# A two-layer encoder trunk on one core: order inside three norms, an adaLN rate, the kept outputs, the last transfers, and the queue of some rows

## The chip, the core and the metric

The kernel runs on one core of one Trainium2 chip. The engines named here are the TensorE (PE, matmuls; PEld is its weight load), the VectorE (DVE), the ScalarE (ACT), GpSimd (POOL) and SyncE (SP), which issues nearly all transfers. The metric is the device time of one execution in microseconds (us); lower is better. Differences of a few us are spoken of, so the runs are repeated.

## The reference

One sequence of 256 tokens, width 2048, two layers, everything in float32. In each layer a vector of six times 2048 values is made from a conditioning vector; its parts shift, scale and gate the two halves of the layer. Cut to what matters:

```python
for l in range(DEPTH):                                   # 2 layers
    mod = cond @ w_ada[l] + b_ada[l]                     # 2048 x 12288
    sh_a, sc_a, g_a, sh_m, sc_m, g_m = split(mod, 6)
    h = rmsnorm(x) * (1 + sc_a) + sh_a
    proj = h @ w_in[l]                                   # all attention inputs
    mix = concat(diff_attention(proj), mla_attention(proj)) @ w_o[l]
    x = x + g_a * mix
    h = rmsnorm(x) * (1 + sc_m) + sh_m
    y = square(relu(h @ w_mlp_in[l])) @ w_mlp_out[l]     # 2048 x 8192 x 2048
    x = x + g_m * y
return rmsnorm(x) * final_norm_g
```

The differential attention adds a bias that depends on the tokens' distance, the same in both layers.

## The kernel before

**Matmuls in parts.** Each weight tile is loaded raw, 1 MB or 768 KB at a time, into a ring of five tiles (`raw`, line 168). `part` (from line 145) makes two tiles of each half: ACT copies it at the precision that PE multiplies fast (`hi`, line 151), and DVE subtracts that from the raw half (`lo`, line 152). Four `hi` and four `lo` tiles exist. Activations are split in the same way. A product is then three matmuls: `hi` by high, `hi` by low and `lo` by high (lines 192 to 194 in `mac`, 213 and 216 in the wide form, 298, 299 and 301 for rows of output, 270 and 272 in `wide_by_k`). So each weight passes SP's queue, ACT and DVE before PE can use it, and the three engines' instructions stand in one fixed order each, mostly that in which the code is written. `behind(a, b)` puts instruction a behind b on its engine where a scheduler could choose otherwise.

**The adaLN rows.** `w_ada` comes as 192 tiles of 1 MB (`ada`, issued at line 346) that use the same ring of five. DVE multiplies each with the conditioning vector and sums it (line 362), 2.28 us apiece; lines 374 and 376 finish a piece of `mod`. How many are fetched beside the weights is set by rates: each call of `weights` adds `self.rate` to a credit and fetches a tile per whole credit (`more_ada`, line 157). The rates are one line of numbers (95); that of layer 0's attention, 1.1, holds through its value stage, the eight weights `w_dv` that `interleave` (line 976) mixes with the second attention. Where a stage needs a part of `mod` that isn't there, `ada_need` fetches and sums it at once.

**The norms.** The very first norm has a function of its own (`first_norm_then_by_k`); its loads, adaLN rows above all, fill the start of the program. The other three go through `norm_then_by_k` (line 707): layer 0's MLP (with `by_k`), layer 1's attention and layer 1's MLP (with `wide_by_k`). The 2048 columns of x are taken in eight pairs of 128. A pair is transposed by PE into a bank (`tx`, line 1125) and copied out (`xT`, line 1134 on ACT or 1132 on DVE); `modulated` scales it on DVE (`ht`, line 684), adds the shift on ACT (`h`, line 687: the high part) and makes the low part on DVE (line 688). Then PE multiplies the pair with its weight tiles into six banks that stay open over all eight pairs. Six banks, one for the norm's roots (`pn`) and one for the transposes make the eight banks of PSUM. In the code, pair 0's h is followed by its weight parts, by its matmuls, and by the transposes of pairs 6 and 7, before pair 1's h is written.

**The gates and the row.** `gate` (line 1061) writes a part of `mod`, one element per partition and column, to DRAM and reads it back as one row broadcast to all partitions, into `self.row` (its tile is called `bias` in the profile). Both transfers are issued on SP's queue (lines 1065 and 1067), the second behind the first one's landing. The same tile holds the attention's bias; layer 0 puts that aside in DRAM (`bias_kept`, line 960) and layer 1 fetches it (line 869). At line 962 x is loaded once more, into the tile that then takes the sums.

**The MLP's outputs.** The 8192 hidden columns are taken in four blocks (`fb`). Each has eight pairs of hidden tiles and then four chunks of 512 output columns for two halves of the tokens (`rows`, 298 to 301). `update` (lines 1076 and 1078) multiplies a result with the gate's row and adds it to x. In layer 0 the gate comes only with block 1, so block 0's eight results are kept (`late`) and go through `update` in one batch ahead of block 1's chunks. `final` (line 1028) does the last chunk of layer 1, the last norm and the output, half by half of the tokens: two scalings on DVE, one on ACT, and two transfers of 512 KB.

Of the kernel before, what the change touches and what calls it, by code (L numbers as in the profile page):

```python
# [16 lines left out]
P = 128  # L17
T = 256
D = 2048
# [78 lines left out]
RATE_A0, RATE_A1, RATE_A2, RATE_K, RATE_K1, RATE_M = 1.1, 0.5, 0.7, 0.6, 0.0, 0.66  # L98
# [3 lines left out]
class Trunk:  # L102
# [33 lines left out]
    def weights(self, src, width=2048):  # L136
        raw = self.raw(src, width)
        half = width // 2
        out = []
        for i in range(2):  # L140
            w, ins = self.part(raw, i, half)
            out.append(w)
        self.more_ada(ins)
        return out

    def part(self, raw, i, half, after=None):
# [4 lines left out]
        self.nc.scalar.activation(hi, v, AF.Copy)  # L151
# [37 lines left out]
    def mac(self, ps, w, c, m, x, first, last, shared=False):  # L189
# [4 lines left out]
        mm(ps, lo, x[0], start=False, stop=last, skip_group_check=shared)  # L194
# [34 lines left out]
    def by_k_weights(self, srcs, n, whole):  # L229

        out = []
        for src in srcs:
# [5 lines left out]
            else:  # L238
                w = self.weights(src, 2 * half)
# [3 lines left out]
    def by_k(self, banks, blocks, xs, k0, nk, n=4, whole=None):  # L243


        for b, (w, half) in enumerate(blocks):
            for i in range(len(w) * half // (n * P)):
                k = k0 + i
                for j in range(n):
# [7 lines left out]
                    else:  # L257
                        self.mac(ps, w[c // half], c % half, P, xs[k], first, last, True)

    def wide_by_k(self, banks, blocks, xs, k0, nk):  # L260
# [4 lines left out]
        for i in range(2 * half // (n * P)):  # L265
# [3 lines left out]
            for j, ps in enumerate(banks):  # L269
                mm(ps.rearrange("p a b -> p (a b)"), part(j, 0), both, start=k == 0, stop=False)  # L270
            for j, ps in enumerate(banks):
                mm(ps[:, 0], part(j, 1), x, start=False, stop=k == nk - 1)  # L272
# [404 lines left out]
    def modulated(self, x, r, k, sh, sc, after=None):  # L677
# [4 lines left out]
        for i, (hi, lo, _) in enumerate(out):  # L682
            c = slice(k + i, k + i + 1)
            ins = nc.vector.scalar_tensor_tensor(t[:, i], x[:, i], sc[:, c], r, ALU.mult, ALU.mult)
            if after is not None:
                self.behind(ins, after)
            self.last_h = nc.scalar.activation(hi, t[:, i], AF.Identity, bias=sh[:, c])  # L687
            ins = nc.vector.scalar_tensor_tensor(lo, t[:, i], sh[:, c], hi.bitcast(F32), ALU.add, ALU.subtract)  # L688
# [18 lines left out]
    def norm_then_by_k(self, l, sh, sc, src):  # L707
# [17 lines left out]
        late = self.last_spread  # L725
        banks = None
        h = []
        for p in range(8):
# [3 lines left out]
            new, ins = self.modulated(x[p], rb, k, self.mod[l, sh], self.mod[l, sc], ins if p == 1 else None)  # L732
            h += new
            if p == 0:
                x += [self.turned(p, late, False, self.last_h) for p in range(4, 6)]
                banks = self.open_banks(6)
            if p:
                blocks = self.by_k_weights([src[p, b] for b in range(2 - l)], 6, False)
            else:
# [5 lines left out]
                blocks = [(parts[2 * b : 2 * b + 2], 768) for b in range(len(raws))]  # L745
            if l == 0:
# [3 lines left out]
            if p == 0:  # L750
                x += [self.turned(p, late) for p in range(6, 8)]
# [630 lines left out]
```

## Time and profile before

| what | value |
|---|---|
| runs shown, median (lowest to highest) | 2208.36 us (2207.84 to 2215.34), 3 runs |
| profiled execution, its own time | 2209.65 us |
| its span from the first instruction to the last | 2207.8 us |
| mean granted clock of TensorE | 0.994 |
| TensorE busy | 2155.4 us |
| VectorE, ScalarE, GpSimd busy | 1595.2, 1143.0 and 1.9 us |
| bytes moved | 594.76 MB, 269 GB/s on the mean |

A row of the timeline gives start and duration in us, the engine, the line of the code, the operation, the output and inputs by name (buffer numbers left out), the shape, how many of them follow one another, and in brackets how long the engine sat idle before and what ended that. A row of waits gives the waiting engine, its output and line, the instruction waited for, then total us, times, and the longest. A row of a stretch gives from:to, the length, then busy us (and instructions) of PE, PEld, DVE, ACT and POOL, the granted clock, the share of the DMA engines and GB/s. Starts of the timeline lie on the axis of the span.

### The profile page before, as it was taken

How to read it: one execution, taken by the hardware profiler on the slowest of the kernel's cores; microseconds unless marked ns; L12 is line 12 of the kernel's file. 1: busy time of each engine (PE TensorE's matmuls, PEld its weight loads, DVE VectorE, ACT ScalarE, POOL GpSimd, SP SyncE). 2: the span in 40 equal slices, each digit the busy share in tenths (PEclk: the TensorE clock that was granted, in tenths of full speed). 3: DMA queues.
4: the chain of work that ended last, by engine and by line, in shares of the span. 5: the costliest groups of instructions: out<-in, count | busy, mean ns of one | idle time of the engine just before them, and what ended most of it. 6: DMA issues, size and time to landing. Idle time of an engine off the chain costs nothing.

```text
span 2207.8 us, 29335 instructions
## 1 busy us (share of the span) xinstructions
PE 2155.4 (98%) x11498; PEld 1865.6 (84%) x11498; DVE 1595.2 (72%) x2122; ACT 1143.0 (52%) x1722; POOL 1.9 (0%) x10
## 2 busy tenths in 40 slices
PE   7999999999999999999999999999999999999998
PEld 6898878888887888888879998888888888888886
DVE  7888778988678878887876876778755555555555
ACT  6555664555454355345454565546545534644643
POOL 0000000000000000000000000000000000000000
PEclk9999999999999999999999999999999999999999
DMA  9988889798887888888967776666875555555552
GB/s 388 421 333 324 269 312 348 277 348 324 321 291 284 339 305 320 326 307 304 333 218 251 260 254 218 251 237 228 282 287 194 191 192 189 191 193 188 191 196 91
DMA packets 94795, 594.76 MB, mean 269 GB/s; under 512 B 17984, under 2 KB 18368, under 8 KB 27840
## 3 DMA queue, kind: packets, MB, share of 16 engines
q1 hardware_dynamic: 94656, 592.88, 73.7%
q8 instruction: 90, 1.47, 0.2%
q14 instruction: 49, 0.40, 0.1%
HBM read 589.66 MB, written 3.18 MB: 269 GB/s over the span
## 4 chain that ended last, share of the span: by engine, by line
PE 91%; DVE 4%; DMA 3%; ACT 1%; issue 1%; SPq 0%; DVEq 0%; ACTq 0%
PE ps L213 18%; PE pr L301 13%; PE pr L298 13%; PE pr L299 13%; PE ps L216 9%; PE pk L256 3%; PE pk L270 2%; PE pk L193 2%; PE pk L194 2%; PE pk L192 2%; PE pv L283 1%; PE pv L282 1%; PE pv L281 1%; PE pk L272 1%; DVE ada L362 1%; DMA raw<-in_w_m 1%
## 5 line engine op out<-in xcount | busy, mean ns | idle before, releaser
L152 DVE TENSOR_TENSOR lo<-raw,hi 128x1024 fp32r<-128x1024 f32 (+1 forms) x714 | 835.0, 1193 | 464.3 <-issue 219.3
L151 ACT ACTIVATE hi<-raw 128x1024 fp32r<-128x1024 f32 (+1 forms) x714 | 733.5, 1036 | 743.1 <-PE pr L299 363.8
L362 DVE SCALAR_TENSOR_TENSOR ada<-ada,cond 128x2048 f32<-128x2048 f32 x192 | 437.9, 2283 | 12.1 <-DMA ada<-in_w_ada 11.4
L213 PE MATMUL ps<-h,hi 128*128 128x512 f32 x1856 | 431.8, 390 | 2.4 <-ACT hi L151 2.4
L213 PEld LDWEIGHTS ps<-h,hi 128*128 128x128 f32 x1856 | 345.1, 188 | 72.2 <-ACT hi L151 2.8
L298 PE MATMUL pr<-hi,hid 128*128 128x512 f32 x1024 | 398.9, 390 | 0.0
L299 PE MATMUL pr<-hi,hid 128*128 128x512 f32 x1024 | 398.7, 389 | 0.0
L301 PE MATMUL pr<-lo,hid 128*128 128x512 f32 x1024 | 254.5, 390 | 5.2 <-DVE lo L152 5.2
L216 PEld LDWEIGHTS ps<-h,lo 128*128 128x128 f32 x1856 | 230.3, 192 | 4.5
L216 PE MATMUL ps<-h,lo 128*128 128x256 f32 x1856 | 231.7, 283 | 0.0
L301 PEld LDWEIGHTS pr<-lo,hid 128*128 128x128 f32 x1024 | 192.5, 188 | 45.7 <-DVE lo L152 5.8
L298 PEld LDWEIGHTS pr<-hi,hid 128*128 128x128 f32 x1024 | 192.5, 188 | 40.3 <-ACT hi L151 0.4
L299 PEld LDWEIGHTS pr<-hi,hid 128*128 128x128 f32 x1024 | 192.4, 188 | 39.8
L1144 ACT ACTIVATE sum<-ps 128x256 f32<-128x256 f32 x110 | 41.7, 381 | 102.2 <-PE ps L216 101.5
L192 PE MATMUL pk<-h,hi 128*128 128x256 f32 x320 | 89.2, 287 | 5.0 <-ACT h L687 5.0
L193 PE MATMUL pk<-h,hi 128*128 128x256 f32 x320 | 91.0, 286 | 0.3 <-DVE h L688 0.3
L194 PE MATMUL pk<-h,lo 128*128 128x256 f32 x320 | 90.8, 286 | 0.0
L256 PE MATMUL pk<-hf,w 128*128 128x256 f32 x384 | 83.9, 379 | 0.0
L256 PEld LDWEIGHTS pk<-hf,w 128*128 128x128 f32 x384 | 72.8, 190 | 9.9
L186 DVE TENSOR_TENSOR hid<-relu,hid 128x256 fp32r<-128x256 f32 x128 | 48.2, 419 | 43.3 <-ACT hid L185 43.3
L1076 DVE TENSOR_TENSOR yg<-pr,bias 128x512 f32<-128x512 f32 x72 | 47.5, 682 | 30.0 <-PE pr L301 30.0
L192 PEld LDWEIGHTS pk<-h,hi 128*128 128x128 f32 x320 | 60.9, 193 | 5.7 <-ACT h L687 5.6
(230 smaller groups left out, 2486.4 us busy)
## 6 DMA issues: line engine op xcount, KB each, us to landing
raw<-in_w_m SPq DMA_DIRECT2D x238, 1024.0 KB, 5.3
ada<-in_w_ada SPq DMA_DIRECT2D x192, 1024.0 KB, 6.2
raw<-in_w_o SPq DMA_DIRECT2D x32, 1024.0 KB, 5.8
raw<-in_w_m SPq DMA_DIRECT2D x24, 768.0 KB, 5.5
raw<-in_w_dv SPq DMA_DIRECT2D x16, 1024.0 KB, 6.2
raw<-in_w_t SPq DMA_DIRECT2D x12, 1024.0 KB, 4.9
w<-in_w_a SPq DMA_DIRECT2D x24, 384.0 KB, 13.5
raw<-in_w_a SPq DMA_DIRECT2D x12, 768.0 KB, 5.4
```

Of the source, the lines that this page charges most:

```text
L151: self.nc.scalar.activation(hi, v, AF.Copy)
L152: ins = self.nc.vector.tensor_tensor(lo, v, hi.bitcast(F32), ALU.subtract)
L192: mm(ps, hi, x[0], start=first, stop=False, skip_group_check=shared)
L193: mm(ps, hi, x[1], start=False, stop=False, skip_group_check=shared)
L194: mm(ps, lo, x[0], start=False, stop=last, skip_group_check=shared)
L213: mm(ps.rearrange("p a b -> p (a b)"), part(w, k, 0), x[2], start=k == 0, stop=False)
L216: mm(ps[:, 0], part(w, k, 1), x[0], start=False, stop=k == nk - 1)
L256: self.nc.tensor.matmul(ps, v, whole[k], start=first, stop=last, skip_group_check=True)
L298: mm(ps, xh[:, c], part(i, 0), start=kq == 0 and i == 0, stop=False)
L299: mm(ps, xl[:, c], part(i, 0), start=False, stop=False)
L301: self.last_mm = mm(ps, xh[:, c], part(i, 1), start=False, stop=kq == 3 and i == 3)
L362: ins = nc.vector.scalar_tensor_tensor(w, w, 1.0, self.cond, ALU.mult, ALU.mult, accum_out=acc[:, i : i + 1])
```

## The change

The change has five parts.

1. In `norm_then_by_k` the h of pair 1 is ordered ahead of the later weight parts on ACT and DVE; the transposes of pairs 6 and 7 move behind the first column of matmuls of pairs 1 and 2; and `wide_by_k` begins its very first product with the `lo` matmuls.
2. The value stage of layer 0 has a rate of its own, 1.6.
3. The kept outputs are no longer updated in a batch: each of block 1's chunks adds the kept one to its own result (`added`), and updates once.
4. `final` does both halves' sums first and writes four transfers of 256 KB a half, two of the eight from ACT's queue.
5. The gates' rows, the bias that is kept and fetched, and the reload of x are issued on GpSimd's queue.

```diff
-RATE_A0, RATE_A1, RATE_A2, RATE_K, RATE_K1, RATE_M = 1.1, 0.5, 0.7, 0.6, 0.0, 0.66
+RATE_A0, RATE_V, RATE_A1, RATE_A2, RATE_K, RATE_K1, RATE_M = 1.1, 1.6, 0.5, 0.7, 0.6, 0.0, 0.66
...
+        if l == 0:
+            self.rate = RATE_V
         self.interleave(
             [val(cg, kq) for cg in range(2) for kq in range(4)],
             mla[6:] + [av[0][0], av[1][0]],
         )
+        if l == 0:
+            self.rate = RATE_A0
...
     def part(self, raw, i, half, after=None, hi_after=None):
...
-        self.nc.scalar.activation(hi, v, AF.Copy)
+        ins = self.nc.scalar.activation(hi, v, AF.Copy)
+        if hi_after is not None:
+            self.behind(ins, hi_after)
...
         for p in range(8):
...
-            new, ins = self.modulated(x[p], rb, k, self.mod[l, sh], self.mod[l, sc], ins if p == 1 else None)
+            new, ins = self.modulated(x[p], rb, k, self.mod[l, sh], self.mod[l, sc], gate)
+            gate = None
...
+                gate = ins, self.last_turn
...
+                order = (self.last_h, ins) if p == 1 else None
+                blocks = self.by_k_weights([src[p, b] for b in range(2 - l)], 6, False, order)
+            if p in (1, 2):
+                x.append(self.turned(5 + p, self.last_mm, False, self.last_h))
...
-            if p == 0:
-                x += [self.turned(p, late) for p in range(6, 8)]
...
-            for j, ps in enumerate(banks):
-                mm(ps.rearrange("p a b -> p (a b)"), part(j, 0), both, start=k == 0, stop=False)
-            for j, ps in enumerate(banks):
-                mm(ps[:, 0], part(j, 1), x, start=False, stop=k == nk - 1)
+            for h in (1, 0) if k == 0 else (0, 1):
+                for j, ps in enumerate(banks):
+                    if h:
+                        mm(ps[:, 0], part(j, 1), x, start=k == 0, stop=k == nk - 1, skip_group_check=True)
...
-            for n, y in enumerate(late):
-                self.update(y.rearrange("p a b -> p (a b)"), n % 2, n // 2)
-            late = []
...
+                    if late:
+                        pss = [self.added(late.pop(0), ps) for ps in pss]
                     self.updates(pss, c, end)
...
+    def added(self, y, ps):
+
+        self.nc.vector.tensor_tensor(y, ps, y, ALU.add)
+        return y
...
-            nc.scalar.activation(self.xr[:, t, :1024], self.xr[:, t, :1024], AF.Copy, scale=r)
-            nc.sync.dma_start(out[:, :1024], self.xr[:, t, :1024])
...
-            nc.sync.dma_start(out[:, 1024:], self.xr[:, t, 1024:])
+            parts = [self.xs_of(t, i) for i in range(4)]
+            outs = [self.io["out"][t, :, 512 * i : 512 * i + 512] for i in range(4)]
+            ins = nc.vector.tensor_scalar(parts[2], parts[2], r, None, ALU.mult)
+            self.behind(ins, ready[1] if t else self.last_x)
+            nc.sync.dma_start(outs[2], parts[2])
...
+            nc.sync.dma_start(outs[3], parts[3])
+            for i in range(2):
+                nc.scalar.activation(parts[i], parts[i], AF.Copy, scale=r)
+                (nc.scalar if t else nc.sync).dma_start(outs[i], parts[i])
...
-        self.nc.sync.dma_start(d.rearrange("k p -> p k"), self.mod[l, g])
+        self.nc.gpsimd.dma_start(d.rearrange("k p -> p k"), self.mod[l, g])
...
-        self.nc.sync.dma_start(self.row, flat.broadcast_to([P, D]))
+        self.nc.gpsimd.dma_start(self.row, flat.broadcast_to([P, D]))
```

The same replacement of `nc.sync` by `nc.gpsimd` is made for `bias_kept` (both ways) and for the two halves of x.

In the norm of layer 0's MLP, ACT's rows behind pair 0's h (the last of it is `h_3570` before and `h_3584` after) read as follows before; `xT` are transposed pairs, `hi` the later weight parts, `h_3700` and `h_3701` pair 1's h:

```order
L687 ACTIVATE h_3570<-ht_3568,mod_81 128x256
L1134 ACTIVATE xT_3582<-tx_3577 128x512
L1134 ACTIVATE xT_3589<-tx_3584 128x512
L151 ACTIVATE hi_3710<-raw_3708 128x768
L151 ACTIVATE hi_3714<-raw_3708 128x768
L151 ACTIVATE hi_3721<-raw_3719 128x768
L151 ACTIVATE hi_3725<-raw_3719 128x768
L1134 ACTIVATE xT_3690<-tx_3685 128x512
L1134 ACTIVATE xT_3697<-tx_3692 128x512
L687 ACTIVATE h_3700<-ht_3699,mod_81 128x256
L687 ACTIVATE h_3701<-ht_3699,mod_81 128x256
```

and after the change:

```order
L698 ACTIVATE h_3584<-ht_3582,mod_81 128x256
L1165 ACTIVATE xT_3596<-tx_3591 128x512
L1165 ACTIVATE xT_3603<-tx_3598 128x512
L698 ACTIVATE h_3700<-ht_3699,mod_81 128x256
L698 ACTIVATE h_3701<-ht_3699,mod_81 128x256
L151 ACTIVATE hi_3710<-raw_3708 128x768
L151 ACTIVATE hi_3714<-raw_3708 128x768
L151 ACTIVATE hi_3721<-raw_3719 128x768
L151 ACTIVATE hi_3725<-raw_3719 128x768
L1165 ACTIVATE xT_3736<-tx_3731 128x512
L698 ACTIVATE h_3811<-ht_3810,mod_81 128x256
```

Pair 1's h moved ahead of four weight parts and of the copies of two transposed pairs, of which one now stands between those parts and pair 2's h (`h_3811`), the other further on.

On DVE the kept outputs (`y`) stood, before, between the two halves' `lo` of one weight tile at the start of block 1's chunks. The first ten rows, behind which nine more updates follow before the next `lo`:

```order
L152 TENSOR_TENSOR lo_6214<-raw_6211,hi_6213 128x1024
L1076 TENSOR_TENSOR yg_6150<-y_4852,bias 128x512
L1076 TENSOR_TENSOR yg_6153<-y_4854,bias 128x512
L1078 TENSOR_TENSOR x<-x,yg_6150 128x512
L186 TENSOR_TENSOR hid_6141<-relu_6138,hid_6141 128x256
L186 TENSOR_TENSOR hid_6142<-relu_6138,hid_6142 128x256
L1078 TENSOR_TENSOR x<-x,yg_6153 128x512
L1076 TENSOR_TENSOR yg_6156<-y_5003,bias 128x512
L1076 TENSOR_TENSOR yg_6159<-y_5005,bias 128x512
L1078 TENSOR_TENSOR x<-x,yg_6156 128x512
```

After the change, the end of the first of the four chunks:

```order
L154 TENSOR_TENSOR lo_6352<-raw_6349,hi_6351 128x1024
L1047 TENSOR_TENSOR y_4859<-pr_6157,y_4859 128x512
L1047 TENSOR_TENSOR y_4861<-pr_6158,y_4861 128x512
L1107 TENSOR_TENSOR yg_6305<-y_4859,bias 128x512
L1107 TENSOR_TENSOR yg_6308<-y_4861,bias 128x512
L1109 TENSOR_TENSOR x<-x,yg_6305 128x512
L1109 TENSOR_TENSOR x<-x,yg_6308 128x512
L154 TENSOR_TENSOR lo_6356<-raw_6349,hi_6355 128x1024
```

The sixteen instructions of the batch are gone, and each chunk has two more, the additions, ahead of its four.

At the program's end DVE's rows before (`rms` is the reciprocal root of a half, `cond` holds the final norm's weights):

```order
L1109 RECIPROCAL rms_18157<-rms_18157 128x1
L1047 SCALAR_TENSOR_TENSOR x<-x,rms_18157,cond 128x512
L1049 TENSOR_SCALAR x<-x,rms_18157 128x512
L1076 TENSOR_TENSOR yg_18625<-pr_18473,bias 128x512
L1078 TENSOR_TENSOR x<-x,yg_18625 128x512
L1109 RECIPROCAL rms_18157<-rms_18157 128x1
```

and after:

```order
L1140 RECIPROCAL rms_18141<-rms_18141 128x1
L1107 TENSOR_TENSOR yg_18604<-pr_18457,bias 128x512
L1109 TENSOR_TENSOR x<-x,yg_18604 128x512
L1071 TENSOR_SCALAR x<-x,rms_18141 128x512
L1074 SCALAR_TENSOR_TENSOR x<-x,rms_18141,cond 128x512
L1140 RECIPROCAL rms_18141<-rms_18141 128x1
```

The second half's update moved ahead of the first half's two scalings.

More of the change, by code (lines that the diff above doesn't have):

```diff
@@ L140, in weights @@
         for i in range(2):
-            w, ins = self.part(raw, i, half)
+            w, ins = self.part(raw, i, half, order and order[1], order and order[0])
             out.append(w)
@@ L144, in weights, with part @@
         return out
-    def part(self, raw, i, half, after=None):
+    def part(self, raw, i, half, after=None, hi_after=None):
         v = raw[:, i * half : (i + 1) * half]
@@ L238, in by_k_weights @@
             else:
-                w = self.weights(src, 2 * half)
+                w = self.weights(src, 2 * half, order)
             out.append((w, half))
@@ L258, in by_k @@
                         self.mac(ps, w[c // half], c % half, P, xs[k], first, last, True)
+                if i == 0 and not whole:
+                    self.last_mm = self.last_mac
     def wide_by_k(self, banks, blocks, xs, k0, nk):
```

51 lines of the change are left out of this document (30 added, 21 removed).

## The prediction

> **What bounds the kernel now.** I read the page's busy times and chain first, then the waits of the TensorE (PE), then the timeline around each of those waits. The page, busy us with the share of the span, and the chain that ended last:
>
> ```profile
> PE 2155.4 (98%) x11498; PEld 1865.6 (84%) x11498; DVE 1595.2 (72%) x2122; ACT 1143.0 (52%) x1722; POOL 1.9 (0%) x10
> PE 91%; DVE 4%; DMA 3%; ACT 1%; issue 1%; SPq 0%; DVEq 0%; ACTq 0%
> ```
>
> PE is busy for 98% of 2207.8 us and carries 91% of the chain. The matmuls stay as they are, so the change can win only from the 52.4 us in which PE idles (2207.8 less 2155.4) and from time at a lower clock. PE's waits (total us, times, longest), those that the change can touch:
>
> ```profile
> PE pr L301 <- DVE lo L152: 5.2, 1, 5.2
> PE pk L192 <- ACT h L687: 5.0, 3, 3.6
> PE pk L270 <- DVE h L688: 4.7, 4, 1.6
> PE ps L213 <- ACT hi L151: 2.4, 1, 2.4
> PE psm L1267 <- DVE sm L1269: 2.1, 2, 1.6
> PE pss L192 <- ACT hi L151: 2.1, 1, 2.1
> ```
>
> They are single waits, each with a place of its own. I went through them in the timeline (start, duration, instruction, idle before it).
>
> **Part 1, the norms ahead of a projection.** Norm of layer 0's MLP, layer 1's attention and layer 1's MLP, PE's rows at the second and third pair:
>
> ```profile
> 420.21 0.66 PE L1125 MATMUL tx<-ident,x 128*128 128x128 f32 x4 [0.86 <-ACT xT L1134]
> 421.95 0.98 PE L192 MATMUL pk<-h,hi 128*128 128x256 f32 x6 [1.08 <-ACT h L687]
> 1140.46 1.67 PE L270 MATMUL pk<-h,hi 128*128 128x512 f32 x6 [0.76 <-DVE h L688]
> 1146.07 0.66 PE L1125 MATMUL tx<-ident,x 128*128 128x128 f32 x4 [0.69 <-ACT xT L1134]
> 1148.33 2.93 PE L270 MATMUL pk<-h,hi 128*128 128x512 f32 x6 [1.60 <-DVE h L688]
> 1495.26 0.66 PE L1125 MATMUL tx<-ident,x 128*128 128x128 f32 x4 [0.69 <-ACT xT L1134]
> 1497.52 1.65 PE L270 MATMUL pk<-h,hi 128*128 128x512 f32 x6 [1.60 <-DVE h L688]
> ```
>
> In all three the transposes of pairs 6 and 7 stand between pair 0 and pair 1, the second waits for ACT to clear its bank, and pair 1 waits for its h, which ACT and DVE reach only after the weight parts. Afterwards the transposes lie one behind each of pairs 1 and 2, and h goes first, so both waits go. Layer 0's MLP: 0.86 + 1.08 = 1.9. Layer 1's attention: 0.69 + 1.60 = 2.3, and the six matmuls took 2.93 where the same six at 1497.52 took 1.65: the clock had dropped, 1.3 more. The 0.76 at pair 0 waits for the low half of h; the changed order begins with six matmuls that read the high half alone, taken at 0.6. Sum 4.2. Layer 1's MLP: 0.69 + 1.60 + 0.6 = 2.9, but the order keeps a sum of one adaLN row ahead of pair 1's scaling:
>
> ```profile
> 1490.78 2.28 DVE L362 SCALAR_TENSOR_TENSOR ada<-ada,cond 128x2048 f32<-128x2048 f32 x1
> ```
>
> It ends at 1493.06, and ht, h on ACT and h on DVE, of 0.4 to 0.5 each, need some 2 us more. PE is through with pair 0 about 1494, since it waits from 1494.57 with four transposes done. About 1.0 is late again; 1.9 is left. The weight parts that now come later are next in line on both engines. They are needed one product after h, so I count nothing for them and cover them in the slack term below.
>
> **Part 2, four more adaLN rows in layer 0's value stage.** Later they need not be forced. Where they are forced now, at pair 7 of the MLP's norm, PE stops:
>
> ```profile
> 477.73 0.86 PE L192 MATMUL pk<-h,hi 128*128 128x256 f32 x5 [3.65 <-ACT h L687]
> 470.00:480.00 10.00, 6.10 (x45) 5.69 (x44) 10.00 (x16) 4.07 (x6) 0.00 (x0) 0.94 0.98 401
> ```
>
> The second row is a stretch: its length, then busy us of PE, weight load, DVE, ACT and POOL, clock, share of the DMA engines, GB/s. DVE is busy for all ten us, with the forced sums, and the clock is at 0.94 on the mean because it drops behind the stop; I price the drop at 1.5 by the one in part 3, whose matmuls can be counted out. Gain 3.7 + 1.5 = 5.2. The price lies in the value stage, a row of the same kind:
>
> ```profile
> 240.00:297.00 57.00, 55.38 (x268) 46.23 (x267) 40.16 (x65) 31.85 (x63) 0.00 (x0) 1.00 0.87 290
> 90.00:120.00 30.00, 30.00 (x144) 26.52 (x143) 18.91 (x27) 6.46 (x12) 0.00 (x0) 1.00 1.02 420
> ```
>
> Four sums of 2.28 lift DVE from 40.2 to 49.3 of 57 us, and four loads of 1.05 MB lift DMA from 290 to 364 GB/s, under the 420 of the second row. Both fit on average, not at each point: cost from 0 (a mere filling of gaps) to 5 (half of the 9.1 us on PE's path), taken at 1, nearer to the gaps.
>
> **Part 3, the kept outputs.** Now sixteen DVE instructions stand in one batch ahead of a weight part for which PE waits:
>
> ```profile
> 692.98 1.29 DVE L1076 TENSOR_TENSOR yg<-y,bias 128x512 f32<-128x512 f32 x2
> 703.39 2.35 DVE L152 TENSOR_TENSOR lo<-raw,hi 128x1024 fp32r<-128x1024 f32 x2
> 704.66 2.08 PE L301 MATMUL pr<-lo,hid 128*128 128x512 f32 x4 [5.19 <-DVE lo L152]
> 706.53 0.63 PE L298 MATMUL pr<-hi,hid 128*128 128x512 f32 x1
> 727.00:749.00 22.00, 22.00 (x99) 18.22 (x98) 18.05 (x19) 8.56 (x9) 0.00 (x0) 1.00 0.90 341
> ```
>
> The wait of 5.19 goes. The four matmuls behind it took 1.87 to the next start against four times the usual 0.225 (22 us by 98 to 99 matmuls), so 1.0 is lost to the clock there, and the matmul after them still shows a long 0.63: 1.5 in all, an estimate. Gain 6.7. In return each chunk of the next feed-forward block gets two additions of about 0.65: DVE goes from 18.05 to 19.4 of the 22 us that a chunk takes, 88%. Cost 0 to 4, taken at 0.5.
>
> **Part 4, the rows off SyncE's queue.** A gate is written out in pieces of 4 bytes and read back; until it has landed, the weight loads behind it crawl. The DMA issues from 610 to 640 (KB each, us to landing), the chain there, PE behind it, the page's row for all such loads, and SyncE's wait:
>
> ```profile
> gate<-mod SPq DMA_DIRECT2D x1, 8.0 KB, 14.2
> 622.20 13.86 DMA raw<-in_w_m
> 637.27 3.92 PE L213 MATMUL ps<-h,hi 128*128 128x512 f32 x16 [2.39 <-ACT hi L151]
> raw<-in_w_m SPq DMA_DIRECT2D x238, 1024.0 KB, 5.3
> SPq L1067 <- DMA gate<-mod: 14.5, 2, 7.7
> ```
>
> 8 KB take 14.2 us and a 1 MB load beside them 13.86, where the median of such loads is 5.3; PE loses 2.4. The same at the first gate costs the 1.6 of the psm wait. Taken from SyncE's ring, I expect the weights to flow past: 4.0.
>
> The bias, kept aside, and the reload of x go along, and no longer stand behind the weight loads of the attention stage. By their own waits (a normed chunk of pair 3, the bias's last write, the last normed chunk) they are free within the first norm, where the second row of part 2 has a DMA share of 1.02. Three transfers of 1.05 MB are 3.15 MB; at 420 GB/s that is 7.5 us of queue ahead of the last adaLN rows of the norm:
>
> ```profile
> 101.62 2.29 DVE L362 SCALAR_TENSOR_TENSOR ada<-ada,cond 128x2048 f32<-128x2048 f32 x1 [7.42 <-DMA ada<-in_w_ada]
> 119.19 0.96 DVE L152 TENSOR_TENSOR lo<-raw,hi 128x768 fp32r<-128x768 f32 x1 [3.11 <-issue]
> 129.22 0.16 DVE L374 SCALAR_TENSOR_TENSOR mod<-macc,vec 128x2 f32<-128x2 f32 x1
> 134.29 0.47 PE L192 MATMUL pk<-h,hi 128*128 128x256 f32 x1
> ```
>
> DVE already waits 7.42 for a row there, and PE begins pair 7 five us after mod with no gap. So lateness of mod shows: 0 (DVE has other pauses to give up) to 9 (7.5 and a clock drop of 1.5). I take 3: with its second pause of 3.1 DVE can make up a part, and a part of the loads waits for buffers anyway.
>
> On GpSimd's queue the clearing of kr now stands behind the return of the kept bias; layer 1's whole first norm lies between that return and the attention that reads both, so I count nothing.
>
> **Part 5, the end**, with DVE and SyncE behind PE's last matmul:
>
> ```profile
> 2197.82 0.75 DVE L1047 SCALAR_TENSOR_TENSOR x<-x,rms,cond 128x512 f32<-128x512 f32 x1
> 2198.89 0.68 DVE L1076 TENSOR_TENSOR yg<-pr,bias 128x512 f32<-128x512 f32 x1
> 2203.21 0.38 SPq L1050 DMA_DIRECT2D out_y<-x  x1
> ```
>
> yg of the second half waits on DVE behind two scalings of the first; now it goes first, 1.07 earlier (2198.89 less 2197.82). The last issue moves 256 KB instead of 512, and from it to the span's end 4.6 us pass now. From 0.5 (half of the move is kept) to 2.3 (the move, and a quarter of the 4.6): 1.6.
>
> **The attention stage of layer 0** is reshuffled by the scheduler: the weight parts stand ahead of two copies on ACT now.
>
> ```profile
> 215.29 0.39 PE L192 MATMUL pss<-lath,hi 128*128 128x256 f32 x1 [2.12 <-ACT hi L151]
> ```
>
> 2.1 plus 1.5 of clock are at stake; other rows may get late, so half: 2 (0 to 4).
>
> **The sum.** Gains: 1.9 + 4.2 + 1.9 + 5.2 + 6.7 + 4.0 + 1.6 + 2 = 27.5. Costs: 1 + 0.5 + 3 = 4.5. A stall that goes exposes the next late thing, as the 1.0 in layer 1's MLP norm; 0.4 for each of seven other places is 3. Net 20. The profiled execution is 2209.65 (span 2207.8 and 1.85 around it), which gives 2189.5; the median of the runs shown is 1.3 lower, so I forecast 2188.
>
> **Rivals.** *The gaps are filled again* (0.18): the feed-forward block at 88% DVE costs its 4, the value stage its 5, the first norm its 9. 27.5 − 18 − 3 = 6.5 is left, 2202: between faster and no change.
>
> *The gate stays a brake* (0.12): if the 4-byte pieces slow the 16 engines themselves and not SyncE's ring, moving them changes nothing. For it: DMA engines that serve both. Against it: SyncE's own wait of 7.7. The 4.0 go, so 2192. The Trainium skill, "DMA: Bandwidth & Descriptors", section "Issuing engines are not separate DMA queues", speaks for this rival: transfers run on the same 16 engines whoever starts them, and a second issuer saves only issue time. By it the sum would be 16 instead of 20; the 14.2 us for 8 KB fit it as well.
>
> *Slower: GpSimd's queue starves* (0.05). The place is the last gate:
>
> ```profile
> L1065 SPq DMA_DIRECT2D gate<-mod x4: 377/407/427, 256.3 to 1584.8; - x4
> 1607.78 1.28 DVE L1076 TENSOR_TENSOR yg<-pr,bias 128x512 f32<-128x512 f32 x2
> ```
>
> From 1584.8 to the first use of the row at 1607.78 are 23 us for two transfers in a row; 9.1 us less of sums ahead (four of 2.28) may give up to 9 more. If GpSimd's two transfers take over 32 us, yg blocks DVE and all weight parts behind it. It must take 32 + 31 = 63 us to eat the 20 and make it 11 slower: 2219.5. Against it: only this row is so near to its use. Nothing in the trace shows GpSimd moving anything, so the price is unknown. The Trainium skill, "SBUF — State Buffer", section "SBUF: two separate sides", warns that GpSimd can't write its descriptors during certain two-port DVE operations; no run here shows it yet.
>
> *Not what it says* (0.05): pair 1's order holds in the listing but h still comes late, because the transposed x of pair 1 or its adaLN rows end last. Part 1 falls from 8.0 to 2: 2194.
>
> **How the numbers follow.** My forecast has 0.60. 0.5% is 11.0 us, about what a measurement of this kernel can tell from no change: faster is below 2197.3, slower above 2219.4. Faster: 0.60, the 0.12 and 0.05 of the two small losses, and none of the refilled gaps, less 0.04 for my sum being too rich: 0.73. Same takes the 0.18, that 0.04 and a half of the starving case: 0.24. Slower: 0.03. The range: at the low end the costs at zero and attention at 4, 27.5 + 2 = 29.5, a little short of it, 2180; at the high end the refilled gaps at 2202 and some loss beyond, 2205.
>
> **What would show it.** Right: the waits at L301, L192 and L270 above gone, no adaLN sum ahead of pair 7, no 13-us weight load near 622, PE's idle near 30 us. Wrong: a new PE wait between 110 and 140; DVE waiting for a row near 1600; waits of PE for lo in the value stage or the next feed-forward block; PE idle as long as before.

## The result and the profile after

The changed kernel takes 2194.63 us (median of 4 runs, 2193.98 to 2199.35) against 2209.89 for the kernel before (4 runs beside them): the ratio is 0.9932, 95% interval 0.9908 to 0.9955. That is 15 us faster; 20 were forecast, and 2194.6 lies in the forecast range of 2180 to 2205. The profiled execution took 2194.0 with a span of 2191.8, which is 16.0 less than the span before.

The page, PE's share and the chain, and PE's waits after the change (as before: total us, times, longest):

```profile
PE 2148.8 (98%) x11498; PEld 1861.3 (85%) x11498; DVE 1590.6 (73%) x2114; ACT 1141.8 (52%) x1724; POOL 11.1 (1%) x22
PE 89%; DMA 5%; DVE 4%; ACT 1%; issue 1%; SPq 0%; ACTq 0%; DVEq 0%
```

```profile
PE psm L1298 <- DVE sm L1300: 6.1, 2, 5.6
PE pk L258 <- DMA w<-in_w_d: 3.6, 2, 2.3
PE psc L1232 <- ACT k L339: 1.5, 1, 1.5
PE pk L278 <- ACT hi L151: 1.3, 1, 1.3
PE pr L309 <- ACT hi L151: 1.0, 1, 1.0
PE ps L215 <- ACT hi L151: 0.8, 2, 0.4
```

The waits of 5.2, 5.0, 4.7 and 2.4 that the forecast had listed, and that of pss with 2.1, are gone or down to 0.8 and less; that of psm has grown. The largest new ones are a wait of 5.6 in the value stage, two for `w_d` in the first norm, and one of 1.5 for a key in the attention stage. PE's busy time fell too, by 6.6: behind the start, and ahead of the end, the granted clock dropped four times before (at 215, 478, 705 and 1148) and drops once now (at 275), and slow matmuls count as busy. PE's idle time is 43.0 (2191.8 less 2148.8), against 52.4 before and the "near 30" that the forecast named as a sign of being right.

To see where the 16.0 lie, I took the start of the same instruction in both traces at eight places. The difference after minus before, and its step from place to place, beside the forecast's terms for that stretch:

| up to | before | after | difference | step | forecast |
|---|---|---|---|---|---|
| first pkr matmul (keys; behind the first norm) | 150.12 | 154.40 | +4.3 | +4.3 | +3 |
| first pv matmul (value stage begins) | 225.90 | 226.24 | +0.3 | −3.9 | −2 |
| last pv matmul of layer 0 | 307.92 | 314.75 | +6.8 | +6.5 | +1 −1.6 |
| last update of the output projection | 405.68 | 413.72 | +8.0 | +1.2 | 0 |
| first update in block 1 of the MLP (the batch's, before, excepted) | 718.42 | 710.52 | −7.9 | −15.9 | −15.7 |
| pn, layer 1's first norm | 1138.34 | 1129.66 | −8.7 | −0.8 | 0 |
| last update of layer 1's projection | 1484.78 | 1471.36 | −13.4 | −4.7 | −4.2 |
| second chunk's update in layer 1's block 0 | 1626.74 | 1611.39 | −15.35 | −1.9 | −1.9 |
| end of the span | 2207.8 | 2191.8 | −16.0 | −0.65 | −1.6 |

The three norms, the forced rows and the kept outputs came out almost to the microsecond. What went wrong lies ahead of the MLP, between 0 and 414 us: there the change lost 8.0, where the forecast's terms (+3 −2 −0.6) made 0.4.

The value stage first. The chain there, GpSimd's queue, and PE at its stop:

```profile
257.31 2.21 DVE ada L373 x2
259.52 0.03 DVE r L1222
259.55 14.59 DMA raw<-in_w_dv
```

```profile
257.61 1.18 POOL L1096 DMA_DIRECT2D gate<-mod  x1 [137.72 <-DVE mod L387]
273.49 0.54 POOL L1098 DMA_DIRECT2D bias<-gate  x1 [14.70 <-DMA gate<-mod]
```

```profile
276.93 1.22 PE L1298 MATMUL psm<-kn,qn 128*128 128x256 f32 x2 [5.61 <-DVE sm L1300]
```

The gate's 8 KB go out at 257.6, now from GpSimd's queue; the weight load issued two us later takes 14.59, lands at 274.14, and all that wait for it stand behind it: `hi`, `lo`, the softmax's reduction on DVE, PE. The gate still is a brake. The first norm, PE's rows for the early part of `w_d`:

```profile
97.63 2.61 PE L258 MATMUL pk<-hf,w 128*128 128x256 f32 x11 [2.27 <-DMA w<-in_w_d]
131.98 7.17 PE L258 MATMUL pk<-hf,w 128*128 128x256 f32 x32 [1.31 <-DMA w<-in_w_d]
```

They follow the transfers of x and of the bias, which GpSimd issued at 66.18, 88.51 and 118.82. At the end DVE, ACT's queue and SyncE, the counterpart of the rows shown of before:

```profile
2182.45 0.69 DVE L1107 TENSOR_TENSOR yg<-pr,bias 128x512 f32<-128x512 f32 x1
2185.18 1.34 ACT L1080 ACTIVATE x<-x,rms 128x512 f32<-128x512 f32 x2 [0.23 <-DVE rms L1140]
2185.94 0.97 ACTq L1081 DMA_DIRECT2D out_y<-x  x2
2186.36 0.33 SPq L1078 DMA_DIRECT2D out_y<-x  x1
```

PE's last matmul ends at 2182.42, so the second half's update follows at once, and the last SyncE issue lies 3.94 behind PE where it lay 5.44 behind. But from it to the end of the span 5.4 us pass instead of 4.6.

### The profile page after: what moved, and what is told of

It is laid out like the page before. It is cut to its first block, busy times and chain, and to the rows that moved or that the text cites. A ratio compares the mean times of both kernels' runs of the same rounds, so it can differ in the third digit from the quotient of the medians.

```text
span 2191.8 us, 29356 instructions
## 1 busy us (share of the span) xinstructions
PE 2148.8 (98%) x11498; PEld 1861.3 (85%) x11498; DVE 1590.6 (73%) x2114; ACT 1141.8 (52%) x1724; POOL 11.1 (1%) x22
## 2 busy tenths in 40 slices
DMA packets 87307, 594.76 MB, mean 271 GB/s; under 512 B 9984, under 2 KB 10368, under 8 KB 20352
## 4 chain that ended last, share of the span: by engine, by line
PE 89%; DMA 5%; DVE 4%; ACT 1%; issue 1%; SPq 0%; ACTq 0%; DVEq 0%
PE ps L215 18%; PE pr L309 13%; PE pr L310 13%; PE pr L312 13%; PE ps L218 9%; PE pk L258 2%; PE pk L278 2%; PE pk L194 2%; PE pk L195 2%; PE pk L196 2%; DMA raw<-in_w_m 2%; DVE ada L373 1%; PE pv L293 1%; PE pv L294 1%; PE pv L292 1%; DMA w<-in_w_d 1%
## 5 line engine op out<-in xcount | busy, mean ns | idle before, releaser
L1107 DVE TENSOR_TENSOR yg<-pr,bias 128x512 f32<-128x512 f32 x64 | 42.5, 685 | 30.0 <-PE pr L312 29.0
```

## The experiments

Theory A: the gate's pieces of 4 bytes hold up the DMA engines themselves, whichever queue issues them; they, with the higher rate, make the value stage's stop, and the early transfers of x and the bias make the first norm's. Theory B: SyncE's ring was the brake, as the forecast's sum had it, and the rate alone fills the value stage. Twelve kernels were run in three groups; each group has its own runs of the kernel before (medians 2209.6, 2209.3 and 2208.5), so each gets its ratio to it, with the 95% interval. The changed kernel has 0.9932. Most ratios are good to 0.0013, some 3 us, that of the changed kernel to 0.0024, some 5 us. The differences in us are between medians; one of 2 or 3 us rests on the traces, not on the times.

**Only the gates back on SyncE's queue.**

```diff
-        self.nc.gpsimd.dma_start(d.rearrange("k p -> p k"), self.mod[l, g])
+        self.nc.sync.dma_start(d.rearrange("k p -> p k"), self.mod[l, g])
...
-        self.nc.gpsimd.dma_start(self.row, flat.broadcast_to([P, D]))
+        self.nc.sync.dma_start(self.row, flat.broadcast_to([P, D]))
```

> The changed kernel (2194.6), with the gates' four pairs of transfers issued on SyncE's queue again. Theory A (the pieces of 4 bytes slow the 16 DMA engines, whoever issues them): the value stage keeps a load of w_dv of over 13 us and a wait of psm of about 5; 2193 to 2197, no change beyond noise. Theory B (SyncE's ring was the brake, part 4 as I priced it): the weight loads get slower again, two waits of together 4 us come back, and the reading back blocks SyncE for 7: 2199 or more.

2191.24, ratio 0.9912 (0.9899 to 0.9924). Neither: it is not slower, as B had it, and in the median even 3 faster, though the intervals overlap. On SyncE the gate stands behind the weight loads in order, and goes out at 277.52 instead of 257.61; in the value stage PE then stops for 1.55 at 305.13 instead of 5.61 at 276.93. GpSimd's queue let the gate go as soon as it was ready, into the middle of the value stage. The first to the last pv matmul take 82.5 here, 88.5 in the changed kernel and 82.0 before; the attention stage ahead of it takes 3.9 longer than in the changed kernel, with a wait for a key of 3.5 instead of 1.5. The engines still slow down beside the gate, as the row below for 277.5 to 291.5 shows, and a load there takes 10.30. So the queue as such didn't spare the loads. That the moment decides what PE loses is argued from the times, since queue and moment changed together.

**Only the bias put aside and x on SyncE's queue, at their old place.**

```diff
-            nc.gpsimd.dma_start(self.bias_kept, self.row)
+            nc.sync.dma_start(self.bias_kept, self.row)
             for t in range(2):
-                nc.gpsimd.dma_start(self.xr[:, t], io["x"][t])
+                nc.sync.dma_start(self.xr[:, t], io["x"][t])
```

> The changed kernel (2194.6), with the bias put aside and x reloaded on SyncE's queue, at the place of the kernel before. Theory A (three early transfers of 1 MB delay the first norm, but the place of x also lets the scheduler order the attention stage otherwise): PE's waits for w_d of 2.3 and 1.3 in the first norm go, 4.0 won; the waits for weight parts near 215 come back, about 4 lost: 2193 to 2196. Theory B (both waits for w_d have another cause): they stay, 2195 to 2199. If the attention stage keeps its order all the same: 2190.6.

2190.81, ratio 0.9912 (0.9897 to 0.9926). PE has no wait for `w_d`, and the keys begin at 150.59 (154.40 in the changed kernel, 150.12 before): the early transfers cost 3.8. The wait of 2.1 near 215 is back, and the value stage begins at 225.91, where it began before. So the 3.9 that the changed kernel won in the attention stage came from the place of x as well, and the two cancel there. Theory A was right about the waits, but the time lies below its 2193 to 2196: the stop in the value stage came out 1.3 shorter, and the rest lies within what the times can tell. PE, in this kernel:

```profile
215.18 0.39 PE L194 MATMUL pss<-lath,hi 128*128 128x256 f32 x1 [2.12 <-ACT hi L151]
282.55 1.22 PE L1298 MATMUL psm<-kn,qn 128*128 128x256 f32 x2 [4.27 <-DVE sm L1300]
```

The stop in the value stage, at 282.55, stays.

**Only the rate of the value stage at 1.1 again.**

```diff
-RATE_A0, RATE_V, RATE_A1, RATE_A2, RATE_K, RATE_K1, RATE_M = 1.1, 1.6, 0.5, 0.7, 0.6, 0.0, 0.66
+RATE_A0, RATE_V, RATE_A1, RATE_A2, RATE_K, RATE_K1, RATE_M = 1.1, 1.1, 0.5, 0.7, 0.6, 0.0, 0.66
```

> The changed kernel (2194.6), with the value stage's rate at 1.1 again. Theory A (the gate's small pieces make the value stage's wait, the rate only decides what stands there): the load of w_dv beside the gate stays over 12 us and psm waits 1.5 to 5; the forced rows before pair 7 of the MLP's norm come back with 3.7 of wait and 1.5 of clock: 2194 to 2200. Theory B (four more rows at the higher rate make the wait): psm's wait goes to under 0.5, 7 won, 5.2 lost: 2193. The trace tells them apart by the load's duration.

2194.6, ratio 0.9934 (0.9921 to 0.9946): as with the higher rate. The trace shows two things that cancel. The value stage's stop is gone (psm waits 0.26, the last pv is at 306.56, 1.4 ahead of before), and the forced rows are back:

```profile
279.15 0.70 PE L1298 MATMUL psm<-kn,qn 128*128 128x256 f32 x2 [0.26 <-DVE sm L1300]
474.02 1.01 PE L194 MATMUL pk<-h,hi 128*128 128x256 f32 x3 [3.65 <-ACT h L698]
633.17 3.92 PE L215 MATMUL ps<-h,hi 128*128 128x512 f32 x16 [1.43 <-ACT hi L151]
```

The load of `w_dv` beside the gate still took 11.83 (261.81 to 273.64), so the brake is there without the rate; what the rate does is to take the slack with which PE bore it. SyncE's issues show that slack: when the gate was written, SyncE had issued five of the stage's eight `w_dv` loads before the change, at the rate of 1.1, and four in the changed kernel, so that the slowed load was the sixth there and the fifth here. This kernel and the kernel before the change also write the gate at the same moment (256.6 and 256.3) and at the same rate, one from GpSimd and one from SyncE: the load beside it takes 11.83 and 13.20, and psm waits 0.26 and 1.62. The two stops differ by 1.4, and the slow load stays with either queue. A's mechanism, with B's size.

**Only the gates in larger pieces.** Each is turned by one transpose on PE, so that it is written in 16 pieces of 512 bytes; queue and all else as in the changed kernel.

```diff
-        self.nc.gpsimd.dma_start(d.rearrange("k p -> p k"), self.mod[l, g])
+        pt = self.bank("gt")
+        self.nc.tensor.transpose(pt[:NK, 0, :P], self.mod[l, g], self.ident)
+        s = self.cp.tile([NK, P], F32, name=f"gs{l}{g}")
+        self.nc.scalar.activation(s, pt[:NK, 0, :P], AF.Copy)
+        self.nc.gpsimd.dma_start(d, s)
```

> The changed kernel (2194.6), with each gate turned by one small transpose on PE and copied by ACT, so that it goes to DRAM in 16 pieces of 512 bytes; all else as it is. Theory A (the small pieces slow the engines): no load of 13 us beside a gate, the wait of psm of 5.6 and some 1.5 of clock behind it go, four transposes cost under 0.3 each: 2187 to 2189. Theory B (the higher rate fills the value stage): psm still waits 4 or more, 2194 to 2196.

2185.43, ratio 0.9888 (0.9876 to 0.9901), even below Theory A's 2187 to 2189. That is 9 less than the changed kernel, with the same rate, and the stretch 255 to 285 shows it; first the changed kernel, then this one (busy of PE, weight load, DVE, ACT, POOL; clock; DMA share; GB/s):

```profile
255.00:285.00 30.00, 24.39 (x104) 19.63 (x103) 18.54 (x32) 11.41 (x25) 1.72 (x2) 0.89 0.94 278
```

```profile
255.00:285.00 30.00, 30.00 (x138) 24.75 (x138) 24.55 (x42) 17.20 (x37) 0.00 (x0) 1.00 0.78 285
```

PE is busy throughout, and the DMA engines move slightly more with a share of 0.78 than they did with 0.94. The gate itself isn't in this stretch any more, since its transpose stands behind the value stage in the code; GpSimd waits 5.80 for its landing, at 318. So this run changes the gate's pieces and its moment at once. What the pieces do can still be told apart, by the stretch from a gate's issue to its landing: first the changed kernel, then the gates on SyncE's queue, then this one.

```profile
257.60:273.00 15.40, 13.73 (x63) 10.96 (x61) 10.36 (x17) 5.19 (x13) 1.18 (x1) 1.00 0.94 180
277.50:291.50 14.00, 14.00 (x67) 11.59 (x66) 8.51 (x16) 9.90 (x20) 0.00 (x0) 1.00 0.69 159
312.00:318.00 6.00, 6.00 (x28) 4.92 (x27) 5.03 (x8) 4.43 (x9) 0.50 (x1) 1.00 0.98 371
```

With pieces of 4 bytes the engines fall to 180 and 159 GB/s, at two moments and from two queues; with 512 bytes they keep 371. How much of the 9 comes from the later moment alone stays open.

**The parts that were priced right: undone one by one.** First the norms, with the three functions as they were (`norm_then_by_k`, `modulated`, `wide_by_k`); the core of it:

```diff
-            new, ins = self.modulated(x[p], rb, k, self.mod[l, sh], self.mod[l, sc], gate)
-            gate = None
+            new, ins = self.modulated(x[p], rb, k, self.mod[l, sh], self.mod[l, sc], ins if p == 1 else None)
...
-            if p in (1, 2):
-                x.append(self.turned(5 + p, self.last_mm, False, self.last_h))
...
+            if p == 0:
+                x += [self.turned(p, late) for p in range(6, 8)]
```

> The changed kernel (2194.6), with the norms ahead of a projection in the order of the kernel before (pair 1's h behind the weight parts, the transposes of pairs 6 and 7 behind pair 0, the first product's high parts first). Theory A (the three norms are worth what part 1 of the forecast says, 1.9 + 4.2 + 1.9): 2202 to 2204, with the six waits at the second and third pair back. Theory B (the weight parts that come later take half of it back): 2198 to 2200.

2202.45, ratio 0.9968 (0.9956 to 0.9981): 7.8 more. The waits are back as they were; PE's rows in layer 1's attention (the first) and its MLP:

```profile
1142.68 1.66 PE L274 MATMUL pk<-h,hi 128*128 128x512 f32 x6 [1.60 <-DVE h L692]
1482.80 2.72 PE L274 MATMUL pk<-h,hi 128*128 128x512 f32 x6 [0.76 <-DVE h L692]
1492.18 1.64 PE L274 MATMUL pk<-h,hi 128*128 128x512 f32 x6 [1.60 <-DVE h L692]
```

The clock dropped in the other norm this time: 2.72 at 1482.80 and not at 1142.68. Theory A.

**The kept outputs in one batch again.**

```diff
+            for n, y in enumerate(late):
+                self.update(y.rearrange("p a b -> p (a b)"), n % 2, n // 2)
+            late = []
...
-                    if late:
-                        pss = [self.added(late.pop(0), ps) for ps in pss]
```

> The changed kernel (2194.6), with the eight kept outputs updated in one batch again. Theory A (the batch delays a weight part by 5.2 and the clock drops for 1.5 behind it, the additions in the chunks cost nothing): one wait of PE for lo of about 5 and 2201 to 2202. Theory B (a busier DVE in the chunks costs something): 2197 to 2199.

2200.49, ratio 0.9966 (0.9954 to 0.9978): 5.9 more, a little under A's figure and above B's.

```profile
701.47 2.07 PE L312 MATMUL pr<-lo,hid 128*128 128x512 f32 x4 [5.19 <-DVE lo L154]
```

The same 5.19, followed by the same slow group.

**The old end.** `final` as it was; its core:

```diff
-            ins = nc.vector.tensor_scalar(parts[2], parts[2], r, None, ALU.mult)
-            self.behind(ins, ready[1] if t else self.last_x)
-            nc.sync.dma_start(outs[2], parts[2])
...
+            x = self.xs_of(t, 2)
+            nc.vector.tensor_scalar(x, x, r, None, ALU.mult)
+            nc.sync.dma_start(out[:, 1024:], self.xr[:, t, 1024:])
```

> The changed kernel (2194.6), with the old end: the first half's scalings ahead of the second half's update, two transfers of 512 KB a half. Theory A (the last issue moves by 1.5, but the last transfer takes longer from its issue to the end, so that 0.65 is left): 2195.2, inside the noise; the trace shows about 5.4 from PE's last matmul to the last issue and 4.6 from there to the end. Theory B (the forecast's 1.6): 2196.2.

2193.13, ratio 0.9932 (0.992 to 0.9945): no difference that the runs can tell. In its trace 9.8 us pass from PE's last matmul to the end of the span; with the new end 8.5 to 9.4 pass in the traces of ten kernels, the changed kernel's 9.4 being the largest. The old end takes 9.8 to 10.0 in three traces, against a middle of 8.75 for the new one. So in the traces the end gains 1.1 to 1.3, between the 0.65 of the one trace and the forecast's 1.6; the times don't show it.

**Turned gates, and x on SyncE's queue.** The two repairs together.

> The changed kernel (2194.6), with each gate turned on PE and written in pieces of 512 bytes, and with the bias and x on SyncE's queue at their old place. Theory A (the two losses are independent): 9.2 from the gates, and 3.4 from the first norm, of which the attention stage's old order may take 2 to 4 back: 2182 to 2185. Theory B (they were the same engines' time, counted twice): 2185 to 2187.

2181.94, ratio 0.9877 (0.9863 to 0.989): 27 us faster than before, and 13 faster than the change as given. PE's waits that are left:

```profile
PE pss L194 <- ACT hi L151: 2.1, 1, 2.1
PE pk L278 <- ACT hi L151: 1.3, 1, 1.3
PE pss L196 <- DVE lo L154: 1.0, 2, 0.5
PE pr L309 <- ACT hi L151: 0.7, 1, 0.7
```

No wait for `w_d` and none of psm above 0.6; the wait of the attention stage's old order is there. Apart, the two repairs gave 9.2 and 3.8; together they give 12.7, so the two losses were independent.

**What the gates cost before the change.** The kernel before, with turned gates alone, on SyncE's queue (the diff is that of the larger pieces, with `sync`).

> The kernel before (2209.3), with nothing changed but each gate: turned on PE, copied by ACT and written in pieces of 512 bytes, on SyncE's queue as it was. Theory A (the pieces of 4 bytes cost what the two waits show, 2.4 and 1.6): 2205 to 2206. Theory B (they cost only where the stages around have more rows to fetch, as at the changed kernel's rate of 1.6, where it was 9): 2208 to 2210. If they cost more than the two waits, 2200 to 2204.

2205.61, ratio 0.9989 (0.9981 to 0.9998): about 3, near the two waits of together 4.0, whose rows are gone. New is a wait of the last gate's transpose, which stands ahead of block 0's chunks in the order and waits for its last adaLN sum:

```profile
1577.48 0.37 PE L1066 MATMUL gt<-ident,mod 128*16 128x128 f32 x1 [2.18 <-DVE mod L376]
```

One more row changed: the batch's wait for lo is 2.5 here and not 5.2, behind a gate that is now written at 686.7, just ahead of the batch. At the end of layer 1's projection this trace is 7.5 ahead, and the last gate takes 3.8 of that back. So turning the gates gave 3 in the kernel before and 9 in the changed one with its higher rate; what the small pieces alone cost in the kernel before, these runs don't tell.

**The rate once the gates are out of the way.** The two repairs with the rate at 1.1.

> The kernel with turned gates and with x on SyncE's queue (2181.9), with the value stage's rate at 1.1 again. Theory A (the higher rate costs nothing once the gate leaves the engines free, and saves the forced rows before pair 7: 3.7 of wait and 1.5 of clock): 2186.5 to 2188. Theory B (the rate only moves the cost): 2181 to 2184.

2191.22, ratio 0.9926 (0.9913 to 0.994): 9 more than with 1.6. The forced rows are back with 3.65 and 0.49, and the last gate's transpose waits 1.81. The higher rate, worth nothing in the change as given, is worth 9 here, even more than A's 5.2. Of the 9.9 between the two traces 1.7 lie ahead of the end of the output projection, 6.1 between it and layer 1's first norm, where the forced rows are, and 2.0 at the last gate.

**All rows on SyncE's queue.** The two repairs, with the gates' transfers and the kept bias's return on SyncE's queue as well.

> The kernel with turned gates and with x on SyncE's queue (2181.9), with the gates' transfers and the kept bias's return on SyncE's queue as well, so that none of these rows is left on GpSimd's. Theory A (the queue as such is worth nothing): 2181 to 2184; SyncE's waits behind the gate's landing, some 2 us each now, are covered by the ring. Theory B (a row that waits on SyncE's queue holds the weights up): 2185 or more, with new waits of PE for hi behind the gates or in layer 1's first norm.

2184.32, ratio 0.9893 (0.988 to 0.9907): 2.4 more, between the two. PE waits three times for `hi` in the output projection, where the gate's row is now issued among its weights:

```profile
364.50 0.50 PE L309 MATMUL pr<-hi,mo 128*128 128x512 f32 x1 [0.96 <-ACT hi L151]
376.57 0.50 PE L309 MATMUL pr<-hi,do 128*128 128x512 f32 x1 [0.90 <-ACT hi L151]
388.77 0.50 PE L309 MATMUL pr<-hi,mo 128*128 128x512 f32 x1 [0.85 <-ACT hi L151]
```

The trace is 2.4 later at the end of the output projection, and the times alone wouldn't tell the two apart. GpSimd's queue is thus worth about 2 for rows that are short to write; none of it comes from the stalls that the forecast priced.

**Two transfers a half in the new order.** The two repairs, with the end's order kept and 512 KB a transfer:

```diff
-            outs = [self.io["out"][t, :, 512 * i : 512 * i + 512] for i in range(4)]
+            out = self.io["out"][t]
...
-            nc.sync.dma_start(outs[2], parts[2])
...
-            nc.sync.dma_start(outs[3], parts[3])
-            for i in range(2):
-                nc.scalar.activation(parts[i], parts[i], AF.Copy, scale=r)
-                (nc.scalar if t else nc.sync).dma_start(outs[i], parts[i])
+            nc.scalar.activation(self.xr[:, t, :1024], self.xr[:, t, :1024], AF.Copy, scale=r)
+            nc.sync.dma_start(out[:, 1024:], self.xr[:, t, 1024:])
+            (nc.scalar if t else nc.sync).dma_start(out[:, :1024], self.xr[:, t, :1024])
```

> The kernel with turned gates and with x on SyncE's queue (2181.9), with the new order at the end but two transfers of 512 KB a half instead of four of 256 KB, the last of them on ACT's queue. Theory A (after the last issue a transfer needs about the same time whatever its size here, so the order alone made the gain): 2181.5 to 2182.5, the stretch from PE's last matmul to the end within 0.3 of the four transfers'. Theory B (small last transfers land sooner): 0.7 to 1.5 longer, 2182.6 to 2183.4.

2182.8, ratio 0.9889 (0.9876 to 0.9903): 0.9 more. From PE's last matmul 9.2 pass to the end, against 8.5; but with the same code the stretch spreads from 8.5 to 9.4, so this doesn't settle whether the smaller transfers add anything to the order.

## Why the prediction was right, and where it was not

**Right: part 1** (1.9 + 4.2 + 1.9 forecast, 7.8 measured by undoing it). The point where the forecast saw a new wait, layer 1's MLP, has one: PE waits 1.3 for `hi` at 1481.84, because the weight parts now stand behind h; with the old order that wait is gone. There the forecast had expected h itself to be late for 1.0 behind an adaLN sum; the size was right, the instruction wrong.

**Right: part 3** (6.7 less 0.5 forecast, 5.9 measured). Nothing in block 1's chunks waits for the additions.

**Right in its gain, mis-sized in its price: part 2.** The forced rows' stop went with its 5.2. The step that failed is the cost of 0 to 5, "taken at 1, nearer to the gaps". It asked whether the sums and the loads fit on average; its estimates of 49.3 us of DVE and 364 GB/s said yes. What broke was the run-ahead: adaLN tiles and weights share the ring of five, so more rows leave fewer weights loaded ahead (four loads issued instead of five), and a load that the gate stretches to 14.59 us arrives late. At the rate of 1.1 the stage is 7.1 shorter (81.4 against 88.5), so that is what the rate cost there beside the small pieces. With the turned gates it cost nothing that shows: the stage takes 79.8 at 1.6 and 80.1 at 1.1. The step of 6.5 in that stretch, against −0.6 in the forecast's sum, is the main error.

**Wrong in its mechanism: part 4's gain.** "Taken from SyncE's ring, I expect the weights to flow past" does not hold. Beside the second gate a load again takes 15.47, here in the changed kernel's chain:

```profile
593.73 15.47 DMA raw<-in_w_m
614.27 8.40 DMA raw<-in_w_m
623.89 2.33 PE ps L215 x9
```

PE lost only 0.44 there, instead of 2.39. The gate, whose adaLN rows were done earlier, is now written at 590.96, as block 0's last chunk ends, and not at 614.23, among block 1's hidden tiles; that this spared PE the rest is argued from the times: in the six kernels that write it with small pieces between 589 and 600, PE waits 0.44 at most, in the one that writes it at 608.7 it waits 1.43, and before, at 614.2, 2.39. So the rival of the brake that stays, which I gave 0.12, was the true mechanism, though the total came out another way than its 2192. The rule of the Trainium skill, "DMA: Bandwidth & Descriptors", section "Issuing engines are not separate DMA queues", which spoke for it, agrees with the trace: a load beside the gate takes 14.59 and 15.47 with GpSimd as issuer, and 13.20 and 13.86 before with SyncE.

**Right in size: the early transfers** (3 forecast, 3.8 by undoing them). The last mod of the first norm is indeed 3.8 later, at 133.05 instead of 129.22, but the two stops of PE, together 3.6, are for `w_d`, which the forecast didn't name: its loads between 60 and 125 took 17.3 instead of 14.0 on the median. The second of them, 1.31 at 131.98, is the new wait between 110 and 140 that the forecast had named as a sign of being wrong. **The attention stage** was taken at 2 in a range of 0 to 4, and gave 3.9. What I had not seen is that both hang on one edit, the place of x.

**The slower rival** did not come. GpSimd's transfers of x landed 9.7 to 10.3 us after their issue; the last gate's row took 26.3, from 1564.32 to DVE's use at 1590.64 with a wait of 0.93, and nothing on PE waited for that; the threshold in the forecast was 32. The Trainium skill warns in "SBUF — State Buffer", section "SBUF: two separate sides", that GpSimd can't write descriptors during certain DVE operations. Here no such stall shows: those transfers' 10 us are those of the 1 MB adaLN loads between 60 and 130 before (median 10.2). Whether DVE ran such operations in that stretch, no view tells.

**The sum.** The forecast's −20 against −16.0 in the span: the value stage was worse by 7.1, the first norm by 1.3, the projection by 1.2 and the end by about 1; the attention stage was better by 1.9, and the rest by 1.6. The slack of 3, meant for stalls that come up behind those that go, paid for a part of it; that the misses went both ways is luck. The terms behind 405 us held, and they alone make the change faster.

## What to carry to other kernels

Terms that rested on a single wait with a row of its own, and on an order of instructions that removes it, came out within half a microsecond here (parts 1 and 3). The term that rested on "it fits on average" was off by 6, and the gate's, which had two such waits but a wrong idea of what slows a load, was wrong in its mechanism. When loads of two kinds share one ring, ask how far ahead the second kind still is, and what the slowest load in that stretch takes. And when a transfer of 8 KB slows its neighbours of 1 MB, change the size of its pieces rather than its queue.

## What the runs showed of the hardware

A gate of 2048 pieces of 4 bytes took 11.3 to 15.6 us to land when SyncE issued it and 12.6 to 16.8 when GpSimd did; in 16 pieces of 512 bytes it took 2.3 to 6.2. Issued from GpSimd, the four gates left 8,000 fewer packets under 512 bytes in the page (9984 against 17984; 18048 with the gates back on SyncE's queue), and were no shorter for it.

A stop of PE doesn't always cost clock. The wait of 2.12 at 215.29 and the one of 1.60 at 1148.33 were followed by slow matmuls; the wait of 2.39 at 637.27 was not, and with the norms' old order in the changed kernel the slow group came at 1482.80 instead. One and the same wait of 2.12, for pss near 215, stands in seven of the kernels: the mean granted clock from 212 to 222 is 0.83 in five of them and 1.00 in the other two (both repairs, and those with all rows on SyncE's queue). In an estimate the 1.5 is a chance, not a sum.
